# A hybrid decoder layer on one core: attention's first head begins two steps later in TensorE's order

## The chip, the core and the metric

The kernel runs on one core of one Trainium2 chip. The time is the device time of one execution in microseconds (us), the median of several runs. TensorE (PE in the profile) does the matrix products, VectorE (DVE) and ScalarE (ACT) the elementwise work and the reductions, GpSimd (POOL) a few small operations, and SyncE (SP) issues nearly all DMA transfers.

## The reference

One layer of a decoder on 512 tokens of width 1024. One input projection feeds three groups of heads side by side, their outputs are joined by one output projection, and a gated channel mixer follows:

```python
h = _rmsnorm(x, attn_norm[l])
proj = h @ w_in[l]
p_nsa, p_rw, p_moba = _split(proj, [N_IN_NSA, N_IN_RWKV, N_IN_MOBA])
o_nsa = _head_rmsnorm(_nsa_mixer(p_nsa, ...), nsa_out_gain[l])
o_rw = _rwkv7_mixer(p_rw, ...)
o_moba = _head_rmsnorm(_moba_mixer(p_moba), moba_out_gain[l])
x = x + jnp.concatenate([o_nsa, o_rw, o_moba], axis=-1) @ w_out[l]
x = x + _conv_glu(_rmsnorm(x, ffn_norm[l]), ffn_w_in[l], ...)
return _rmsnorm(x, final_norm)
```

The first group (six heads of 64) is attention with a selected, a windowed and a compressed branch; at 512 tokens the selected and the windowed branch are both plain causal softmax attention, with keys `ks` and `kw`. The second (four heads) is a recurrence with a matrix state, done in chunks of 64 tokens. The third (six heads) is block-sparse attention.

## The kernel before

All work of the first half is written as streams, Python generators that emit instructions and then `yield` a number. `merge` (L1035) keeps a due time for every stream, takes the stream that is due first and can go on, lets it emit one step, and adds the number that it yields to its due time (L1049). A stream that yields `None` is waiting for a condition and is tried again. The instructions so emitted, in this order, are the written order of every engine's queue; the order seen in the trace can differ from it by a little where instructions of two steps are mixed. The numbers are the planner's own units: a projection group of three products yields `CW` = 1.25, an attention step `CATT` = 2.5, a step of the recurrence 3.45 or 3.57 (or half).

The streams that matter here:

- `w_stream` (L1091) does the input projections in the order of `ORDER`: ..., `nv`, `q0`, `cv`, `ck`, `hv`, `q1`, `kw`, ... Each projection is eight groups of three products (`mm3`, L240 to L242: the operands are split into a high and a low part, `whi` and `wlo` for the weights, and three of the four products are summed). A weight unit is split by ScalarE (L211) and VectorE (L212). After the eighth group the result is taken from PSUM; for `q0` that is `evac_q` (L694): VectorE scales it into P (L696), ScalarE rounds it to the high part of the query tile `qt` (L701) and VectorE computes the low part (L702). `cv` and `ck` are taken over by `blocks` (L881), and `hv` is the product `ph` (L917, L918) that uses the blocks of `cv`.
- `rw_pair` (L347) is the recurrence, for two pairs of heads. Its steps here: the small products of L455 with the masks GA and GR that VectorE puts on them (L461, then NM, R and Nc); the inverse of 16 by 16 blocks on VectorE (L494, L496), which goes out and comes back through DMA (L503, L505) and is spread to DvT and Dv (L508); the products of L533 with Y (L573).
- `att_stream` (L1239) goes through `HEADS`: nine items of two halves (`par`). A half waits for its query, keys and values (L1252), and then `soft` (L774) emits four steps, one for each 128 tokens: two products into the bank `s` (L784, L785), the row minimum on VectorE (L788), the exponential on ScalarE (L791), and `yield CATT`. The first half of the first item needs `q0`, the second half needs `q1`, which comes after `cv`, `ck` and `hv`.

PSUM has eight banks; a step that needs one waits with `want` until the count of live banks allows it.

Of the kernel before, what the change touches and what calls it, by code (L numbers as in the profile page):

```python
# [24 lines left out]
CW, CRW0, CRW1, CATT, CVAL, CFIN, CCMP, CCA, RWLAG = 1.25, 3.45, 3.57, 2.5, 1.28, 4.05, 3.17, 1.69, 0  # L25
# [66 lines left out]
def hybrid_layer(ctx: ExitStack, tc: tile.TileContext, xT, cst, cols, lora, fgain, wA, wVn, cw1,  # L92
# [10 lines left out]
    def mark(label):  # L103
        MARKS.append((label, nc.cur_bb.bb.instructions[-1].name))
# [18 lines left out]
    def r2(name, shape=(128, 512), dt=F32):  # L123
        return sb.tile(list(shape), dt, name=name, bufs=cap(name))
# [135 lines left out]
    for z in SEQ:  # L260
# [13 lines left out]
        for k, i in new:  # L274
            n = sum(o[1] == i for o in order1)
# [498 lines left out]
    def soft(qt, kk, par, sums, mid):  # L774
        kh, kl, lo = kk
        two, three = r2("prob"), r2("prob")
        pt_ = two[:, 384:512], mid[:, par * 256:par * 256 + 256], two[:, 0:384], three
        Ps = []
        for i in range(NT):
            n = (i + 1) * 128  # L780
            yield from want()
            s_ = bank("s")
            qs = slice(i * 128, (i + 1) * 128)
            pe.matmul(s_[:, 0:n], qt[:, qs], kh[:, 0:n], start=True, stop=False)  # L784
            pe.matmul(s_[:, 0:n], qt[:, qs], kl[:, 0:n], start=False, stop=True)  # L785
            P = pt_[i]
            m = sm("m", 1)
            dve.tensor_tensor_reduce(out=P, in0=s_[:, 0:n], in1=con("cmask")[:, 512 - n:512], scale=1.0,  # L788
                                     scalar=3e38, op0=OP.add, op1=OP.min, accum_out=m)
            done()  # L790
            act.activation(P, P, AF.Exp, bias=m, scale=-1.0, accum_out=sums[:, i, par:par + 1])  # L791
            Ps.append(P)
            yield CATT
        return Ps
# [399 lines left out]
    def sums_tile():  # L1194
        return sm("sums", 8).rearrange("p (t h) -> p t h", h=2)
# [10 lines left out]
    def fin_nsa(j, b, OPt, sums, ob):  # L1206
        mark(f'fnsa{j}.{b}')
        c = sm("coef", 8)
        cv = c.rearrange("p (t h) -> p t h", h=2)
        dve.reciprocal(cv, sums)  # L1210
        o1 = 6 * j + b
        dve.tensor_tensor(cv, cv, gates[:, :, o1:o1 + 4:3], op=OP.mult)
        t = yield from scaled(OPt, c)
        ob.append(t)
        if len(ob) < 2:
            return
        while not cadone[0]:
            yield None
        yield CFIN
        at('ob').tensor_tensor(ob[0], ob[0], ob[1], op=OP.add)  # L1220
        yield from want()
        oc = bank("oc")
        for i in range(NT):
            pe.matmul(oc[:, i * 128:(i + 1) * 128], PT[j][:, i, :], Vbd[j], start=True, stop=True)
        yield CFIN
        dve.tensor_tensor(ob[0], ob[0], oc, op=OP.add)
        done()
        yield CFIN
        yield from finish_pair(ob[0], col("nsa_gain", j), j)

    def fin_moba(j, OPt, sums):
        mark(f'fmoba{j}')
        r = sm("coef", 8)
        dve.reciprocal(r, sums.rearrange("p t h -> p (t h)"))
        t = yield from scaled(OPt, r)
        yield CFIN
        yield from finish_pair(t, col("moba_gain", j), 5 + j)

    def att_stream():  # L1239
        for kind, j, b in HEADS:  # L1240
            fold = ENG[f"F{kind}{j}{b}"] == 'p'
            OPt, sums = (r2("OPt"), r2("OPt") if fold else None, fold), sums_tile()
            if b < 2:
                ob = []
            while len(queue) > QMAX:
                yield None
            Ps, vs, mid = [], [], r2("prob")
            for par in range(2):
                h = 2 * j + par
                if kind == "n":  # L1250
                    kk = (ks, kw)[b - 1]
                    while qn[h] is None or not kk or not vn:  # L1252
                        yield None
                    q_, k_, v_ = qn[h], kk[h // 3], vn[(b - 1) * 2 + h // 3]
                else:
                    while j not in mq or j not in mk or j not in mv:
                        yield None
                    q_, k_, v_ = mq[j][par], mk[j][par], mv[j][par]
                mark(f'soft{kind}{j}.{b}.{par}')
                vs.append(v_)  # L1260
                P = yield from soft(q_, k_, par, sums, mid)
                Ps.append(P)
            fin = fin_nsa(j, b, OPt, sums, ob) if kind == "n" else fin_moba(j, OPt, sums)
            queue.append((Ps, vs, OPt, fin, f'{kind}{j}.{b}'))
        queue.append(None)
# [14 lines left out]
    spawn(rw_run(0))  # L1280
    spawn(cmp_attention())
    spawn(att_stream())
    spawn(val_stream())
    merge()
# [267 lines left out]
```

## Time and profile before

| | |
|---|---|
| median of 3 runs | 731.04 us (730.73 to 731.48) |
| the profiled execution | 731.48 us, its span in the trace 729.4 us |
| TensorE busy | 705.4 us, 97% |
| VectorE busy | 627.0 us, 86% |
| ScalarE busy | 415.3 us, 57% |
| GpSimd busy | 30.8 us, 4% |

The busy shares are means over stages with different limits. The stage that the change touches is read by windows of time, by the waits of one engine, and by the order of time of one engine. In the order of time, a row gives start and duration in us, the engine, the line, the operation, the tile written and read, and how many records are merged; in brackets stands how long the engine was idle before it and what ended that.

### The profile page before, as it was taken

The page shows a single profiled execution, that of the slowest core. Times are in us where ns is not written, and L with a number is a line of the kernel's source. Part 1 is how long each engine was busy: PE and PEld are TensorE (multiplying, and loading weights), DVE is VectorE, ACT ScalarE, POOL GpSimd, SP SyncE. Part 2 cuts the span into 40 slices and gives each one's busy share as a digit, 9 for nine tenths or more (in the row PEclk, how much of TensorE's full clock was granted, in tenths as well). Part 3 has the DMA queues.
Part 4 walks back from the last instruction along what each step waited for, and adds up shares of the span by engine and source line. Part 5 has one row for each costly group of instructions (what it writes and reads, how often), then busy time and mean ns, then how long its engine had stood idle before and what let it go on. Part 6 is the DMA issues. An engine that isn't in the chain of part 4 may idle for free. (4 is left out here: it accounts for less than half of the span.)

```text
span 729.4 us, 13565 instructions
## 1 busy us (share of the span) xinstructions
PE 705.4 (97%) x5156; PEld 613.6 (84%) x5156; DVE 627.0 (86%) x1377; ACT 415.3 (57%) x862; POOL 30.8 (4%) x46
## 2 busy tenths in 40 slices
PE   9999988899999999999999999999999999999995
PEld 6777867678788788888899899999999999998884
DVE  6579679878897999797999999999999999999804
ACT  8475434465656877774766546455564555657403
POOL 4010100000000000011000000000000000000001
PEclk9989989999999999999999999999999999999999
DMA  9622021513110022024246333323333333346003
GB/s 328 193 87 80 13 50 49 140 65 117 44 44 30 1 59 73 30 72 145 74 144 218 97 107 102 116 87 102 97 108 101 102 103 110 98 126 201 1 1 115
DMA packets 44800, 69.86 MB, mean 96 GB/s; under 512 B 10688, under 2 KB 12352, under 8 KB 44736
## 3 DMA queue, kind: packets, MB, share of 16 engines
q1 hardware_dynamic: 44016, 67.95, 29.4%
q10 hardware_dynamic: 720, 1.06, 0.4%
q8 instruction: 40, 0.66, 0.4%
q14 instruction: 24, 0.20, 0.1%
HBM read 64.40 MB, written 4.59 MB: 95 GB/s over the span
## 5 line engine op out<-in xcount | busy, mean ns | idle before, releaser
L1301 ACT CAST ah<-S 128x512 fp32r<-128x512 f32 x88 | 54.5, 621 | 57.6 <-DVE S L1296 57.6
L240 PE MATMUL mm<-xh,whi 128*128 128x512 f32 x152 | 69.6, 458 | 0.0
L241 PE MATMUL acc<-dn,dn 128*128 128x512 f32 (+1 forms) x173 | 64.3, 372 | 0.0
L242 PE MATMUL acc<-dn,dn 128*128 128x512 f32 (+1 forms) x173 | 63.8, 371 | 0.0
L242 PE MATMUL mm<-xh,wlo 128*128 128x512 f32 x152 | 61.8, 406 | 0.0
L241 PE MATMUL mm<-xl,whi 128*128 128x512 f32 x152 | 61.5, 404 | 0.0
L1302 DVE TENSOR_TENSOR al<-S,ah 128x512 fp32r<-128x512 f32 x88 | 58.7, 682 | 0.7 <-ACT ah L1301 0.6
L791 ACT ACTIVATE prob<-prob,fixed 128x128 f32<-128x128 f32 (+1 forms) x72 | 40.5, 563 | 28.5 <-DVE fixed L788 26.5
L240 PE MATMUL acc<-dn,dn 128*128 128x512 f32 (+1 forms) x173 | 54.9, 371 | 0.0
L211 ACT CAST whi<-wraw 128x512 fp32r<-128x512 f32 x70 | 42.6, 618 | 19.8 <-PE mm L241 14.1
L212 DVE TENSOR_TENSOR wlo<-wraw,whi 128x512 fp32r<-128x512 f32 x70 | 47.3, 682 | 3.6 <-PE mm L242 2.2
L240 PE MATMUL pB<-bh,ah 128*128 128x256 f32 x172 | 50.1, 291 | 0.1
L242 PE MATMUL pB<-bh,al 128*128 128x256 f32 x172 | 48.6, 283 | 1.1 <-DVE al L1302 1.0
L242 PE MATMUL pC<-bh,al 128*128 128x256 f32 x172 | 48.5, 282 | 0.3 <-DVE al L1302 0.3
L240 PE MATMUL pC<-bh,ah 128*128 128x256 f32 x172 | 48.5, 282 | 0.2 <-ACT ah L1301 0.2
L241 PE MATMUL pB<-bl,ah 128*128 128x256 f32 x172 | 48.3, 281 | 0.0
L241 PE MATMUL pC<-bl,ah 128*128 128x256 f32 x172 | 48.1, 280 | 0.0
L1302 DVE TENSOR_TENSOR al<-wraw,ah 128x512 fp32r<-128x512 f32 x66 | 43.4, 681 | 0.0
L823 ACT CAST ph<-pt 128x512 fp32r<-128x512 f32 (+3 forms) x72 | 29.7, 425 | 23.3 <-PE pt L816 22.4
L788 DVE CUSTOM_DVE_ANT_0 prob<-s,early 128x128 f32<-128x128 f32 (+1 forms) x72 | 34.7, 483 | 6.6 <-PE s L785 5.0
L1301 ACT CAST ah<-wraw 128x512 fp32r<-128x512 f32 x66 | 36.8, 618 | 1.4 <-DVE x L1135 1.3
L241 PEld LDWEIGHTS acc<-dn,dn 128*128 128x128 f32 x173 | 32.6, 188 | 5.3 <-DVE dn L1365 0.2
(400 smaller groups left out, 2211.8 us busy)
## 6 DMA issues: line engine op xcount, KB each, us to landing
wraw<-in_wF_dram SPq DMA_DIRECT2D x88, 256.0 KB, 2.7
wraw<-in_wG_dram SPq DMA_DIRECT2D x44, 256.0 KB, 3.0
wraw<-in_wA_dram SPq DMA_DIRECT2D x38, 256.0 KB, 3.0
xr<-in_xT_dram SPq DMA_DIRECT2D x16, 256.0 KB, 4.1
wraw<-in_cw_dram SPq DMA_DIRECT2D x16, 256.0 KB, 3.3
wraw<-in_wO_dram SPq DMA_DIRECT2D x16, 256.0 KB, 2.6
fraw<-in_wA_dram SPq DMA_DIRECT2D x8, 256.0 KB, 5.2
x2d<-x2o SPq DMA_DIRECT2D x8, 256.0 KB, 3.3
```

Of the source, the lines that this page charges most:

```text
L211: act.copy(hi[:, :w], raw)
L212: dve.tensor_tensor(lo[:, :w], raw, hi[:, :w].bitcast(F32), op=OP.subtract)
L240: pe.matmul(o, ah, bh, start=first, stop=False)
L241: pe.matmul(o, ah, bl, start=False, stop=False)
L242: pe.matmul(o, al, bh, start=False, stop=last)
L788: dve.tensor_tensor_reduce(out=P, in0=s_[:, 0:n], in1=con("cmask")[:, 512 - n:512], scale=1.0, scalar=3e38, op0=OP.add, op1=OP.min, accum_ ...
L791: act.activation(P, P, AF.Exp, bias=m, scale=-1.0, accum_out=sums[:, i, par:par + 1])
L823: act.copy(h, t_[:, 0:n])
L1301: act.copy(h, src)
L1302: at(f'L{i}').tensor_tensor(l, src, h.bitcast(F32), op=OP.subtract)
```

## The change

When the first half of the first item has its operands, `att_stream` yields `2 * CATT` = 5.0 units once before it emits its first step. Nothing else is written differently, and no instruction is added or removed.

```diff
                     while j not in mq or j not in mk or j not in mv:
                         yield None
                     q_, k_, v_ = mq[j][par], mk[j][par], mv[j][par]
+                if (kind, j, b, par) == ("n", 0, 1, 0):
+
+                    yield 2 * CATT
                 mark(f'soft{kind}{j}.{b}.{par}')
                 vs.append(v_)
                 P = yield from soft(q_, k_, par, sums, mid)
```

## Rows read from the trace of the kernel before

**Rows 1.** Windows: length, busy us (records) per engine, granted clock, DMA share, GB/s.

```profile
92.60:140.00 47.40, 39.53 (x482) 31.89 (x483) 40.64 (x112) 19.72 (x44) 0.39 (x3) 0.89 0.25 66
140.00:700.00 560.00, 554.81 (x4043) 492.81 (x4042) 512.17 (x1092) 335.29 (x710) 14.96 (x9) 1.00 0.29 92
```

**Rows 2.** Waits of TensorE, 92 to 140 us: total us, times, longest.

```profile
PE s L784 <- DVE qt L702: 3.3, 1, 3.3
PE ph L918 <- DVE wlo L212: 2.5, 2, 2.1
PE rw L533 <- DVE Y L573: 1.7, 1, 1.7
...
```

**Rows 3.** TensorE in order of time, around the first head's first two steps.

```profile
92.19 0.38 PE L455 MATMUL rw<-AR,bb 64*64 64x128 f32 x2
95.91 0.47 PE L784 MATMUL s<-kk,qt 128*128 128x128 f32 x1 [3.34 <-DVE qt L702]
...
96.52 0.49 PE L455 MATMUL rw<-AR,bb 64*64 64x128 f32 x3
...
97.58 0.79 PE L240 MATMUL mm<-xh,whi 128*128 128x512 f32 x1
...
99.03 0.63 PE L240 MATMUL mm<-xh,whi 128*128 128x512 f32 x1
...
100.31 0.41 PE L784 MATMUL s<-kk,qt 128*128 128x256 f32 x1
...
100.86 1.59 PE L533 MATMUL rw<-DvT,R 64*64 64x64 f32 x32
```

**Rows 4.** VectorE in order of time, 86 to 105 us.

```profile
91.50 0.76 DVE L508 TENSOR_TENSOR DvT<-Nc,early 128x256 f32<-128x256 f32 x2 [4.78 <-DMA Nc<-s]
...
93.25 0.69 DVE L696 SCALAR_TENSOR_TENSOR P<-mm,early 128x512 f32<-128x512 f32 x1
...
95.17 1.41 DVE L702 TENSOR_TENSOR qt<-P,qt 64x512 fp32r<-64x512 f32 x2
...
97.69 0.42 DVE L461 TENSOR_TENSOR GA<-rw,early 128x256 f32<-128x256 f32 x1 [0.76 <-PE rw L455]
98.03 0.41 DVE L461 TENSOR_TENSOR GR<-rw,early 128x256 f32<-128x256 f32 x1
...
100.97 0.42 DVE L788 CUSTOM_DVE_ANT_0 prob<-s,early 128x256 f32<-128x256 f32 x1 [1.53 <-PE s L785]
...
104.44 0.42 DVE L461 TENSOR_TENSOR GA<-rw,early 128x256 f32<-128x256 f32 x1 [2.10 <-PE rw L455]
```

**Rows 5.** Windows, columns as in rows 1: behind the stall, VectorE's full stretch, its end.

```profile
97.60:100.30 2.70, 2.70 (x9) 2.13 (x7) 1.75 (x5) 0.00 (x0) 0.00 (x0) 0.50 0.00 0
...
104.40:131.40 27.00, 22.50 (x301) 18.41 (x301) 25.59 (x71) 10.74 (x26) 0.39 (x3) 1.00 0.17 45
...
131.50:134.70 3.20, 3.20 (x43) 2.59 (x43) 3.20 (x13) 2.70 (x6) 0.00 (x0) 0.67 0.52 161
```

**Rows 6.** TensorE in order of time, the same kinds of work at full clock.

```profile
60.01 0.45 PE L455 MATMUL rw<-AR,bb 64*64 64x128 f32 x8
...
61.05 0.50 PE L240 MATMUL mm<-xh,whi 128*128 128x512 f32 x1
...
105.12 0.34 PE L784 MATMUL s<-kk,qt 128*128 128x384 f32 x1
...
105.47 0.39 PE L240 MATMUL mm<-xh,whi 128*128 128x512 f32 x1
...
107.41 1.15 PE L533 MATMUL rw<-Dv,QT 64*64 64x64 f32 x32
108.49 0.50 PE L240 MATMUL mm<-xh,whi 128*128 128x512 f32 x1
...
109.29 0.40 PE L240 MATMUL mm<-xh,whi 128*128 128x512 f32 x1
...
109.98 0.39 PE L240 MATMUL mm<-xh,whi 128*128 128x512 f32 x1
```

## What the change should do to the time

> **What bounds the kernel now.** I read the table by stages first, to see which engine is full and where. From 140 to 700 us TensorE is busy 554.81 of 560.00 us at full clock [rows 1]: whatever time TensorE is ahead when it reaches 140 it keeps, because the work behind it is the same and is fed by engines that are ahead by the same amount. From 92.6 to 140 it is busy only 39.53 of 47.40, at a mean clock of 0.89. So the stage around the first head is where idle TensorE time can be removed.
>
> Second, the waits of TensorE in that stage. The longest, 3.3 us, is the first head's first product (L784), which waits for the query tile qt; the others are 2.5 for weights' low parts (wlo) and 1.7 for Y, all on VectorE [rows 2].
>
> Third, TensorE's order of time. After 18 of the 32 small products of the second recurrence pair (L455; 92.19 is the last of these rows) it stands still until 95.91, then does the first head's product, and only then the other 14 (96.52 is their first row) [rows 3]. Those 14 and the projection behind them do not need qt. The clock in the stretch after it is 0.50, the 1.2 GHz level [rows 5], and a group of three projection products takes 1.45 there (97.58 to 99.03) against 0.80 and 0.69 at full clock (108.49 to 109.29 to 109.98) [rows 3, 6].
>
> Fourth, why qt is late: VectorE's own order of time. It sits 4.78 us on a DMA that brings the inverse back for the first pair, then works off what queued up behind: DvT, Dv, P of the query at 93.25, and qt, which ends at 95.17 + 1.41 = 96.58 by the merged row (its first half is what TensorE waits for) [rows 4].
>
> **The change, part by part.** The yield puts the first head's stream 2 x 2.5 = 5.0 planner units later. A projection group costs 1.25 of them, so the four steps move by four groups each: the first step goes to where the third was (105.12), the second to where the fourth was, and the other two among the first groups of the next projection. The second half of this head waits for q1, which lies well beyond; from there the stream is again at its old place. So just four steps move.
>
> Each moved step issues two products on TensorE, a row minimum with its read on VectorE, an exponential with its read on ScalarE. No DMA is among them, so SyncE's and GpSimd's queues are not passed. Nothing is added or removed: the gain or loss is in waits and clock only.
>
> *TensorE, removed.* The stall, 3.34 by the row of L784 [rows 3]. Then the slow stretch after it: two projection groups 1.45 + 1.28 instead of 0.80 + 0.69, the 32 products of L533 1.59 instead of 1.15, the remaining 14 of L455 1.06 instead of 14/32 of 1.04 = 0.46 [rows 3, 6]: 5.38 - 3.10 = 2.28. The two moved products took 0.61 and 0.55; a larger one at full clock takes 0.35 (105.12 to 105.47), so they are cheaper by 0.46 in their new places. Together 3.34 + 2.28 + 0.46 = 6.1 us.
>
> *TensorE, does the first product wait again?* In the new order TensorE stands at 92.6 with 0.46 of L455, then two groups (0.80, 0.69), L533 (1.15), a group (0.80), the second L455 set (1.04), a group (0.80): it comes to the first product at about 98.3. The query is ready at 96.6, so 1.7 us of cover. If VectorE were later by more than that, the wait would return with the excess only. The second L455 set would stand at 96.5; should it get the PSUM banks of the first, it waits until VectorE has read these, about 96.6 + 4 x 0.34 = 98.0 (the spacing 97.69 to 98.03 and on). That is bounded by 0 and 1.5; I take 0, since it is less than TensorE's surplus over VectorE below.
>
> *VectorE, which decides how much of 6.1 survives.* In 104.4 to 131.4 VectorE is busy 25.59 of 27.00, and it is TensorE that waits [rows 2, 5]. So in that stretch TensorE's lead is cut down to VectorE's. VectorE is not faster before 96.6: its backlog runs without an idle time from P to qt [rows 4]. What it gains is the idle time it had because TensorE stood or ran slowly: 0.76 before the first GA, 1.53 before the second row minimum, 2.10 before the second GA set [rows 4], 4.39 us. With the new order the first GA set is ready at 93, the second at 97.5, and both moved row minima come after products that TensorE does at 98.3 and some 2 us later, where VectorE still has GA, NM, R and weights to do. So I take all three as removed: 4.4. Bounds: if the row minimum still meets its product too early, 1.53 stays, and the gain is 2.9; if also the other idle time of the full stretch closed, 27.00 - 25.59 = 1.41, it is 5.8. The value is near the middle, and follows the three named waits.
>
> *ScalarE* is busy 10.74 of 27.00 there [rows 5]; the four exponentials cost nothing where they go, and their results are used only after q1. If that cover were gone they would cost their own time, under a microsecond each.
>
> **The sum.** The profiled execution took 731.48, its span 729.4. Span 729.4 - 4.4 = 725.0, plus the 2.1 outside it, 727.1; that execution lay 0.44 above the median 731.04, so the median after is **726.6**.
>
> What is late next: with 6.1 of lead on TensorE and 4.4 on VectorE, TensorE meets the wait for Y (1.7 now) about 1.7 us earlier in relation, and it grows to about 3.4.
>
> **The rivals.**
>
> *The clock falls at the longer wait.* The stall of 3.34 was followed by the 0.50 clock; the stretch that holds the wait of 1.7 shows 1.00, and the stretch from 131.5, right behind the wait of 2.1 for weights, shows 0.67 [rows 3, 5]. If the wait for Y grows to 3.4 the same fall would follow there, at the price just worked out, 2.28 + 0.46 = 2.7, and if none of it hid behind the later waits on VectorE, the result is 726.6 + 2.7 = **729.3**. Against it: there are 2.5 us of waits for weights on VectorE behind it [rows 2], in which a slow TensorE loses nothing. The Trainium skill, "TensorE: Matmul & The Clock Gate", section "HAM oscillation", says that an engine which idles while it waits for data is put back to half rate and starts its next work slow; the trace agrees (3.34 idle, then 0.50), and by that rule this rival, at 729.3, is the outcome.
>
> *All of TensorE's gain survives.* If VectorE's full stretch hides slack, for instance because what TensorE waits for can be done earlier in VectorE's queue: 731.0 - 6.1 = **724.9**. For it: 1.41 us idle in the stretch. Against it: 25.59 of 27.00 busy.
>
> *Nothing changes.* The product of L784 stands in the middle of the L455 set, so the finished order is not only the written one; what places it may put it early again, before qt is ready: **731.0**. Against it: L784 would then have to pass four projection groups that are ready.
>
> *Slower.* VectorE's queue is served in order. If a moved row minimum stands there ahead of its product, everything behind it (GA, NM, blocks, weights) waits, in the stretch where VectorE decides. The price of one such meeting is the 1.53 that the second row minimum shows now; all four would cost 6.1, of which 4.4 is paid by the gain: 731.0 + 1.7 = **732.7**. It decides from four meetings of 1.1 on; below that the kernel is still faster. Against it: TensorE is 1.7 ahead of VectorE in the new order, so products come first.
>
> **How the numbers follow.** Forecast 726.6 (its own range, from 2.9 and 5.8: 725.2 to 728.2): 0.58. All survives, 724.9: 0.12. Clock, 729.3: 0.13. Nothing, 731.0: 0.08. Slower, 732.7: 0.09. The range leaves out the last two and little at the lower end: 724.5 to 729.6, 0.8 in all. A measurement of this kernel tells about 0.2%, 1.5 us, from no change: faster below 729.6 is 0.58 + 0.12 + somewhat over half of the clock case, 0.78; same is the rest of that and the fourth case, 0.13; slower 0.09.
>
> **What would show it.** Right: L455 with its 32 products unbroken before 93; L784 first at some 98 with no wait on qt; clock 1.00 from 92.6 to 105; VectorE without the 0.76, 1.53 and 2.10; TensorE's wait for Y longer than 1.7; the first group of q1 some 4.4 earlier than now; the same distances from there to the end. Wrong: a wait at L784 or at the second L455 set; new idle time of VectorE ahead of a row minimum; a clock below 1 behind the wait for Y; or a lead at q1 that is lost later, between 140 and 420.

## The result, and the profile after

The kernel after takes 725.67 us (median of 6 runs, 724.04 to 726.89), the kernel before on the same chip 730.47 (6 runs, 728.79 to 731.48): a ratio of 0.9938, 95% interval 0.9923 to 0.9954. The gain is 4.8 us; forecast were 4.4. The profiled execution of after took 725.59, its span is 723.5. Single executions of one kernel differ by several microseconds (the kernel before ran from 726.6 to 732.8 in all its executions), so below a time is a median, and what an edit did is read from the stage where it lies.

That stage can be measured between two marks that stand in every kernel: the last products ahead of the stage (the second pair's L433) and the products with Dv of the second pair (L533), behind the first head. First TensorE of the kernel before, then of the kernel after; columns are start, duration, engine, line, operation and tile, count, and in brackets the wait with what ended it.

```profile
90.04 1.02 PE L433 MATMUL rw<-rb__956,early 128*128 128x512 f32 x2
...
148.19 1.15 PE L533 MATMUL rw<-Dv,QT 64*64 64x64 f32 x32
```

```profile
88.94 1.02 PE L433 MATMUL rw<-rb__956,early 128*128 128x512 f32 x2
...
91.30 0.40 PE L455 MATMUL rw<-AR,kb 64*64 64x128 f32 x8
...
95.19 0.45 PE L455 MATMUL rw<-AR,bb 64*64 64x128 f32 x8
...
97.02 0.22 PE L784 MATMUL s<-kk,qt 128*128 128x128 f32 x1
...
99.58 0.38 PE L784 MATMUL s<-kk,qt 128*128 128x256 f32 x1 [0.80 <-DVE fixed L788]
...
112.80 1.96 PE L533 MATMUL rw<-TA,Y 64*64 64x128 f32 x32 [1.62 <-DVE Y L573]
...
124.77 0.38 PE L918 MATMUL ph<-wlo,bhl 128*128 128x256 f32 x1 [2.27 <-DVE wlo L212]
...
141.50 1.15 PE L533 MATMUL rw<-Dv,QT 64*64 64x64 f32 x32
```

The stage is 148.19 - 90.04 = 58.15 us long before and 141.50 - 88.94 = 52.56 after: 5.6 shorter. After was 1.1 ahead already at the first mark, which is no work of the change. The set of L455 runs through, the first head's first product at 97.02 waits for nothing, and a new wait stands ahead of the second step's product: 0.80 for the row minimum of the first step.

The waits of TensorE from 92 to 140 us in after, to be set against [rows 2]: the 3.3 is gone, the other two are as they were.

```profile
PE ph L918 <- DVE wlo L212: 2.7, 2, 2.3
PE rw L533 <- DVE Y L573: 1.6, 1, 1.6
PE s L784 <- DVE fixed L788: 0.8, 1, 0.8
...
```

VectorE of after in the same stretch answers [rows 4]. It still waits 4.72 us for the inverse, but from there on no row has a wait: the first GA follows qt at once, the second set follows a weight unit, and the first row minimum stands behind it.

```profile
90.39 0.76 DVE L508 TENSOR_TENSOR DvT<-Nc,early 128x256 f32<-128x256 f32 x2 [4.72 <-DMA Nc<-s]
...
91.97 0.68 DVE L696 SCALAR_TENSOR_TENSOR P<-mm,early 128x512 f32<-128x512 f32 x1
...
93.88 1.41 DVE L702 TENSOR_TENSOR qt<-P,qt 64x512 fp32r<-64x512 f32 x2
95.30 0.42 DVE L461 TENSOR_TENSOR GA<-rw,early 128x256 f32<-128x256 f32 x1
...
97.91 0.41 DVE L461 TENSOR_TENSOR GA<-rw,early 128x256 f32<-128x256 f32 x1
...
99.24 0.28 DVE L788 CUSTOM_DVE_ANT_0 prob<-s,early 128x128 f32<-128x128 f32 x1
```

Windows of after, columns as in [rows 1]. Where the clock was 0.50 [rows 5] it is 1.00, and the whole stretch to 140 has 0.96 for 0.89 (0.93 in a second trace of before, below). Only behind the wait of 2.27 for a weight is it still low (0.66 from 125 to 130, before 0.67).

```profile
92.60:140.00 47.40, 41.91 (x525) 33.11 (x525) 44.59 (x123) 22.51 (x48) 0.38 (x3) 0.96 0.31 85
...
97.60:100.30 2.70, 1.90 (x18) 1.22 (x18) 2.70 (x10) 0.50 (x2) 0.00 (x0) 1.00 0.00 0
92.60:105.00 12.40, 11.60 (x135) 8.76 (x136) 12.29 (x31) 6.04 (x12) 0.00 (x0) 1.00 0.14 34
...
125.00:130.00 5.00, 5.00 (x49) 4.10 (x49) 4.92 (x17) 2.69 (x6) 0.00 (x0) 0.66 0.57 179
```

### The profile page after: what moved, and what is told of

It is laid out like the page before. It is cut to its first block, busy times and chain, and to the rows that moved or that the text cites. A ratio compares the mean times of both kernels' runs of the same rounds, so it can differ in the third digit from the quotient of the medians.

```text
span 723.5 us, 13563 instructions
## 1 busy us (share of the span) xinstructions
PE 701.6 (97%) x5156; PEld 610.4 (84%) x5156; DVE 626.7 (87%) x1377; ACT 415.5 (57%) x862; POOL 30.4 (4%) x46
## 4 chain that ended last, share of the span: by engine, by line
PE 72%; DVE 16%; ACT 4%; DMA 4%; issue 2%; POOL 1%; SPq 0%; POOLq 0%; DVEq 0%; ACTq 0%
PE mm L240 6%; PE mm L241 6%; PE mm L242 6%; PE acc L241 5%; PE acc L242 5%; PE acc L240 5%; PE pB L240 3%; PE ot L804 3%; PE pB L242 3%; PE pB L241 2%; PE pC L240 2%; PE pt L816 2%; PE pC L241 2%; PE pC L242 2%; PE pA L241 2%; PE pA L242 2%
```

## The experiments

Times are medians of the kernel, of the kernel before measured beside it, and their ratio with its interval. The stage is the length between the two marks in the profiled execution.

| kernel | time | before | ratio | stage |
|---|---|---|---|---|
| before | | | | 58.15 |
| before, again | 730.29 | 729.34 | 1.0008 [0.9989, 1.0026] | 57.41 |
| after | 725.67 | 730.47 | 0.9938 [0.9923, 0.9954] | 52.56 |
| after, again | 725.38 | 729.66 | 0.9938 [0.9919, 0.9958] | 52.54 |
| one step | 724.09 | 730.45 | 0.9912 [0.9894, 0.9930] | 55.03 |
| one step, again | 725.07 | 729.66 | 0.9929 [0.9905, 0.9953] | 55.49 |
| four steps | 726.96 | 730.45 | 0.9956 [0.9939, 0.9973] | 54.57 |
| before, stall filled with products | 728.31 | 730.45 | 0.9970 [0.9957, 0.9984] | 55.83 |
| before, first DvT and Dv on GpSimd | 724.59 | 730.45 | 0.9922 [0.9907, 0.9937] | 51.68 |
| after, first DvT and Dv on GpSimd | 723.89 | 729.66 | 0.9919 [0.9898, 0.9941] | 51.41 |
| after, both pairs' DvT and Dv on GpSimd | 723.40 | 729.59 | 0.9915 [0.9895, 0.9934] | 52.54 |
| after, half of the block sums on GpSimd | 724.74 | 729.66 | 0.9928 [0.9908, 0.9949] | 52.06 |
| after, three more additions on VectorE | 729.27 | 729.59 | 0.9997 [0.9979, 1.0015] | 55.60 |
| before, the same three additions | 727.22 | 729.59 | 0.9964 [0.9948, 0.9980] | 56.46 |

**Both kernels once more.**

> The changed kernel once more, for a comparison on the same chip as the one-step delay. Expected as measured, 4 to 5.5 us faster than before.

> The kernel before, unchanged, once more, for a second trace of it: the other kernels' traces run 0.6 to 2.5 us ahead of the first trace of it already at 90 us, ahead of the place of the change, and the kernel before with additions on VectorE came out 2.4 us faster than without. Theory (the stall and the half clock behind it belong to the order, and how long each lasts differs from execution to execution with the return of the inverse by DMA): this trace too has a wait for qt of 2.8 to 3.4 us at the first product and a stretch of clock below 1.00 behind it, and its lead over the first trace at 138 us stands where it stood at 90 us, give or take 1.7 us (the length of the slow stretch). Rival (the slow stretch is a rare event of the first trace): the wait is there, the clock behind it is 1.00 throughout, and the lead grows by 2.0 us or more between 90 and 105 us.

After repeats itself: 52.54 for 52.56 us. Before does not quite. TensorE of its second execution, and the clock behind the stall (window, TensorE busy, granted clock, DMA share, GB/s):

```profile
95.24 0.35 PE L784 MATMUL s<-kk,qt 128*128 128x128 f32 x1 [3.98 <-DVE qt L702]
...
99.54 1.15 PE L533 MATMUL rw<-DvT,R 64*64 64x64 f32 x32
```

```profile
97.00:98.00 1.00, 1.00 (x3) 0.50 0.00 0
...
99.00:100.00 1.00, 1.00 (x19) 1.00 0.00 0
```

The stall is longer (3.98 for 3.34, above the 2.8 to 3.4 expected), the slow stretch shorter: the products of L533 take 1.15 here and took 1.59 [rows 3]. From the first product to the third it is 9.21 us in the first trace (95.91 to 105.12 [rows 3, 6]) and 8.11 in this one (95.24 to 103.35). The same work in the same order at full clock stands in the kernel with the first DvT and Dv on GpSimd (below); its first and third product:

```profile
91.21 0.33 PE L784 MATMUL s<-kk,qt 128*128 128x128 f32 x1 [0.53 <-DVE qt L702]
...
97.81 0.34 PE L784 MATMUL s<-kk,qt 128*128 128x384 f32 x1
```

That is 6.60, so the half clock cost 2.6 and 1.5 us in two executions of one kernel. The stall's own length goes with the DMA: the inverse is sent out and fetched back, and the second issue follows the first by 3.45 us in the first trace, by 3.87 in this (84.26 to 88.13), and by 3.09 in before with additions (below), where the stall is 2.92; it is 3.26 and 3.06 in the two of after. The theory of this run holds: stall and slow stretch belong to the order, their lengths do not. The mean of the two stages, 57.8, is the better base: the change shortens the stage by 5.2.

**One step and four instead of two.**

```diff
-                    yield 2 * CATT
+                    yield CATT        (four steps: 4 * CATT)
```

> The stream waits one step (2.5 units) instead of two; the rest is as in the changed kernel. My theory (the query tile comes late because VectorE's queue stands behind a DMA, and what TensorE gains is kept as far as VectorE gains): TensorE reaches the first product 1.3 to 1.5 us before the query is ready, so a wait of about that length comes back, too short for the clock to fall; VectorE still loses its three idle times (0.76, 1.53, 2.10), so nearly all the gain stays: 3.5 to 5 us faster than before, at most 1 us behind the changed kernel. Rival (TensorE's own time is what counts): the returned wait is paid in full, 1.4 us slower than the changed kernel.

> The one-step delay once more. In its first trace the wait for the query came back with 1.84 us and the clock fell behind it, and that execution was the slowest of its six. If the fall of the clock is by chance at a wait of this length, a second trace may show the wait with the clock at 1.00 and the time near the median of the first (724.1), even with or 1 us ahead of the changed kernel; if it falls at every wait of this length, the trace shows 0.50 again and the time is 1 to 2 us behind the changed kernel.

> The stream waits four steps (10 units). My theory: the query is ready long before, no wait is left to remove, so the time is that of the changed kernel within 1 us. Rival (the place of the steps counts in itself, the later the better or the worse): another 2 us or more in either direction.

With one step the first product still comes too early, and the clock falls behind its wait, which the first expectation had ruled out. TensorE of the second of these runs, and its window behind the wait (columns as in [rows 1]):

```profile
94.19 0.33 PE L784 MATMUL s<-kk,qt 128*128 128x128 f32 x1 [2.04 <-DVE qt L702]
...
96.92 0.71 PE L455 MATMUL rw<-AR,bb 64*64 64x128 f32 x8
```

```profile
96.00:98.00 2.00, 2.00 (x23) 1.35 (x25) 1.76 (x6) 0.81 (x3) 0.00 (x0) 0.50 0.03 8
```

Both traces have the wait (1.84 and 2.04) and the half clock behind it, and a stage 2.5 to 2.9 us longer than after's. Farther on both wait 1.92 for Y. What follows that wait differs; TensorE and a window of the first trace, then of the second:

```profile
116.05 3.57 PE L533 MATMUL rw<-TA,Y 64*64 64x128 f32 x32 [1.92 <-DVE Y L573]
...
117.00:119.00 2.00, 2.00 (x24) 2.00 (x22) 1.97 (x7) 0.58 (x1) 0.12 (x1) 0.50 0.09 35
```

```profile
114.92 1.96 PE L533 MATMUL rw<-TA,Y 64*64 64x128 f32 x32 [1.92 <-DVE Y L573]
...
116.00:118.00 2.00, 2.00 (x30) 1.69 (x24) 1.94 (x8) 1.65 (x3) 0.13 (x1) 1.00 0.02 8
```

One kernel, one wait of the same length, and once the half clock, once the full. The 1.6 us that L533 takes longer do not show in the stage (55.03 for 55.49): TensorE waits 1.0 less for weights behind it (2.2 for 3.2).

Yet the times of the two series are not longer than after's (ratio 0.9912 and 0.9929 against 0.9938, the intervals overlap), so neither case of the second expectation came in whole. Part of the difference lies behind the stage (below, in the step on the distances to the end). And the traced execution of the first series is not a typical one: it is the slowest of its six (726.58), with a mean granted clock of 0.990, where the other five have 0.994 or 0.995 and take 722.55 to 725.36. Whether those had the slow stretches no trace shows. Which of the two delays is better the times do not tell.

With four steps the first product waits for nothing, and the queue of steps falls later instead, among the block products. TensorE and a window of that kernel:

```profile
111.16 0.43 PE L917 MATMUL ph<-whi,bhl 128*128 128x256 f32 x1 [1.78 <-DVE stmp L494]
...
112.67 3.68 PE L533 MATMUL rw<-TA,Y 64*64 64x128 f32 x32 [0.65 <-DVE Y L573]
```

```profile
115.00:118.00 3.00, 3.00 (x22) 2.67 (x19) 2.81 (x8) 1.32 (x3) 0.00 (x0) 0.50 0.00 0
```

TensorE reaches the block products and Y sooner than VectorE has them, waits 1.78 and 0.65 us, and the clock falls: L533 with TA takes 3.68 for 1.96 in after. That is the prediction's rival of the clock, with another wait than the one that it named. The stage is 2.0 us longer than after's, where no difference was expected, and the ratio 0.9956 is the smallest gain of the delays.

**Stall or clock: the stall filled.** The kernel before, with 14 products ahead of the first head's product, whose result nobody reads:

```diff
+                if (kind, j, b, par) == ("n", 0, 1, 0):
+                    yield from want()
+                    fill = bank("s")
+                    for _ in range(14):
+                        pe.matmul(fill, xh[0][:, 0:128], vn[0].rearrange("p t a d -> p t (a d)"), start=True, stop=True)
+                    done()
```

> The order of before, with 14 products of 512 columns that nobody reads put in front of the first head's first product (3.2 us at full clock), so that TensorE works while the query is late. It takes the clock's share of the gain from the stall's. My theory: the stall goes to under 1 us of idle, the clock stays at 1.00, the work itself is not done earlier at the stall but is not slowed after it; the slow stretch costs 2.3 to 2.7, of which VectorE lets 1 to 2.5 through: 728 to 729.5 with before at 730.5. Rival (the fall of the clock costs nothing, only the stall does): as before or up to 0.6 us slower. Rival (the clock is nearly all of it): as the changed kernel.

TensorE of it:

```profile
89.36 3.43 PE L1263 MATMUL s<-vn,xh 128*128 128x512 f32 x14
93.45 0.33 PE L784 MATMUL s<-kk,qt 128*128 128x128 f32 x1 [0.66 <-DVE qt L702]
```

The useful work comes hardly earlier, and all 32 products of L455 now stand behind the first product, where before has 14 of them; but the clock is 1.00 there, and the stage falls from 57.8 to 55.8. That agrees with the 2.6 and 1.5 found above for the half clock, 2.1 in the mean. So about 2 of the 5.2 us are the clock's; the stage of after is 3.3 shorter than this one, and that part needs useful work in the stall's place. The times differ by 2.1 as well (730.45 to 728.31), but that is no second proof: in this trace the first mark comes 0.9 and 2.2 earlier than in the two of before, and the rest behind the stage is 1.3 longer (582.5), both outside the stage.

**The cause ahead of the stall.** The order of before, but DvT and Dv of the first pair, which wait for the DMA, on GpSimd:

```diff
-        for src, dst, eng in ((XX, DvT, dve), (X, Dv, at('dv'))):
+        for src, dst, eng in ((XX, DvT, dve if p else pool), (X, Dv, dve if p else pool)):
```

> The order of before, but the four products that spread the returned inverse of the first pair to DvT and Dv run on GpSimd, so VectorE does not stand behind their DMA. My theory: the query's P starts at about 90.2 instead of 93.25, qt is ready for the first product at about 92.5, the wait of 3.3 shrinks to under 1 us, the clock stays at 1.00, and the kernel is 4.5 to 7 us faster than before with every step in its old place. Rival (what counts is where the steps stand in TensorE's order): within 1 us of before.

VectorE and GpSimd of it, in order of time:

```profile
88.36 0.69 DVE L696 SCALAR_TENSOR_TENSOR P<-mm,early 128x512 f32<-128x512 f32 x1 [3.43 <-PE mm L242]
```

```profile
90.00 1.63 POOL L508 TENSOR_TENSOR DvT<-Nc,early 128x256 f32<-128x256 f32 x2 [9.45 <-DMA Nc<-s]
```

P now waits for its own operand, not behind the DMA; the wait at the first product is 0.53, the clock 1.00, the stage 51.7 (6.1 shorter), the time 5.9 below before. So qt was late because P stood behind DvT on VectorE; with that cured, the order of before is as good as the new one. The 6.1 are not the wait's alone: the edit also takes four operations, two rows of 0.76 us [rows 4], off VectorE.

The change and this edit together:

> The changed kernel with DvT and Dv of the first pair on GpSimd as well, so both remedies for the same wait at once. My theory (both take away the same wait): the two gains don't add; TensorE has no wait left to lose at the first product, VectorE is rid of four short products (1.4 us) and of 1 us of backlog: 0 to 2 us faster than the changed kernel, 724 to 726. Rival (two separate gains): they add, 4.8 + 5.9, about 720.

The stage is 51.4, 0.3 shorter than with the edit alone and 1.1 shorter than with the change alone. The gains do not add (5.2 and 6.1 would be 11.3), as expected of two remedies for the same idle time.

**Who decides behind the stall: more work for VectorE.** Three additions of 512 columns behind the first GA and GR of the second pair, whose result nobody reads, in after and in before:

```diff
-                done()
+                done(); [dve.tensor_tensor(r2('pad', (128, 2, 2, 2, CH)), GA[0], GR[0], op=OP.add) for _ in range(3 * p * par * (2 - c0) // 2)]
```

> The changed kernel with three additions of 512 columns added on VectorE, behind the first GA/GR set of the second pair; nobody reads their result, and all else stands in the same order on every engine. By the rows of other 512-column operations they cost 0.60 to 0.68 us each, 1.8 to 2.0 together. Theory (since the change VectorE has no idle time between 92 and 131 us, and its order of work there sets how early the second half comes): VectorE is later by 1.8 to 2.0 us from there, TensorE's waits for VectorE (Y, wlo) take that up, the lead over the kernel before falls from 5.6 to 3.6 to 3.8 us by 138 us, and the time is 1.5 to 2.0 above that of the changed kernel, about 727.2. Rival (what was won is TensorE's alone, VectorE had room left): the lead stays at 5.2 or more and the time within 0.5 of 725.4.

> The kernel before with the same three additions on VectorE at the same place, behind the first GA/GR set of the second pair; nobody reads their result. Theory: the additions stand where VectorE waits 2.10 us for the second GA/GR set, so that wait shrinks to 0.1 to 0.3 us, what follows from 104.4 us on is where it was, and the time is that of the kernel before within 0.5 us (730.0 to 731.0); together with the same additions in the changed kernel (1.5 to 2.0 us there) this says that the idle time of VectorE, and not TensorE's alone, is what the change won. Rival (additions on VectorE cost the same wherever they stand): 1.8 to 2.0 us slower, 732.3.

In after: VectorE, then TensorE.

```profile
95.41 0.68 DVE L464 TENSOR_TENSOR pad<-GA,GR 128x512 f32<-128x512 f32 x1
...
102.50 0.69 DVE L573 TENSOR_TENSOR Y<-rw,Dv 128x512 f32<-128x512 f32 x1 [0.79 <-PE rw L533]
```

```profile
99.83 0.50 PE L784 MATMUL s<-kk,qt 128*128 128x256 f32 x1 [2.36 <-DVE fixed L788]
...
100.47 1.97 PE L533 MATMUL rw<-Dv,QT 64*64 64x64 f32 x32
```

In before: VectorE at the second GA set.

```profile
99.95 0.69 DVE L464 TENSOR_TENSOR pad<-GA,GR 128x512 f32<-128x512 f32 x1
100.55 0.42 DVE L461 TENSOR_TENSOR GA<-rw,early 128x256 f32<-128x256 f32 x1
```

The additions take 1.8 us (three of 0.60, from start to start). In before they lie in the wait of 2.10 ahead of the second GA set, which is gone in this trace: the stage is 56.5, not longer than before's 58.2 and 57.4, as the theory had it. In after the stage grows by 3.0, more than their own 1.8: the row minimum of the first step comes later, TensorE's wait for it grows from 0.80 to 2.36, the clock falls (L533 takes 1.97 for 1.15), and VectorE then waits for TensorE in its turn (0.79, and 0.62 for cP). So VectorE had idle time there before the change and has none after it: that idle time is what the change won.

Both expectations of time missed. After with the additions is 3.6 to 3.9 us slower than after (1.5 to 2.0 expected); the extra is the new waits with the clock, and 0.9 behind the stage (582.97 us from the second mark to the end). Before with the additions is not level with before but 2.4 us faster. Its trace shows a shorter stall (2.92) and a short slow stretch (8.11 from first to third product, as in before's second trace), and 1.4 less behind the stage (579.7 for 581.1), which goes back to one wait for a transfer far from the additions (below, in the step on the distances to the end). A stage 1.3 shorter and a rest 1.4 shorter are the gain; neither is shown to come from the additions.

**What bounds next.** Half of the block sums (L896) of after on GpSimd, `'blk': 'p'` for `'blk': 'v'` in the table of engines:

> The changed kernel with every second of the 16 additions at L896 (0.57 us each) on GpSimd: 8 x 0.57 = 4.6 us less for VectorE in its full stretch. My theory (VectorE decides what is kept there): TensorE's waits on VectorE in that stretch (1.6 for Y, 2.7 for weights) shrink and the kernel gets 1.5 to 4 us faster than the changed one. Rival (TensorE or the recurrence's chain decides): within 0.7 us of the changed kernel.

VectorE, GpSimd and TensorE of it:

```profile
109.26 0.57 DVE L896 TENSOR_TENSOR blk<-cP,fixed 64x248 f32<-64x248 f32 x1
109.76 0.66 DVE L496 TENSOR_TENSOR X<-X,stmp 64x39 f32<-64x39 f32 x1
110.45 1.07 DVE L896 TENSOR_TENSOR blk<-cP,fixed 64x248 f32<-64x248 f32 x1
```

```profile
108.86 2.30 POOL L896 TENSOR_TENSOR blk<-cP,fixed 64x248 f32<-64x248 f32 x2
```

```profile
135.13 1.15 PE L533 MATMUL rw<-DvT,R 64*64 64x64 f32 x32 [1.27 <-DVE DvT L508]
```

The waits for weights (2.7 in after) are gone, but the stage is only 0.5 shorter than after's and the time 0.6 below it, where 1.5 or more had been expected. While GpSimd works, operations of VectorE take 1.07 for 0.57 and 0.66 for 0.2; TensorE now waits 1.27 us for the second pair's inverse, and longer than in after for the first row minimum (1.16 for 0.80). The lengthened rows and the recurrence's chain with its round trip by DMA are what stands against the gain; the share of each is not shown.

DvT and Dv on GpSimd for both pairs, in the changed kernel (`pool` for both engines in the line above):

> The changed kernel with the spreads DvT and Dv (L508) on GpSimd for both pairs, so VectorE waits for neither return of an inverse by DMA. With the first pair alone on GpSimd the lead was 6.7 us. Theory (VectorE's order of work decides, and its second wait for the DMA of 1.9 us at 134 us blocks P of the second head too): up to 1.9 us more, if TensorE's waits for wlo and for DvT behind 128 us don't take it: a lead of 7 to 8.5, time 722 to 724. Rival (behind 130 us TensorE waits for the inverse itself, which GpSimd spreads 0.9 us later than VectorE would): lead as with the first pair alone, 6.2 to 6.8, time 723.5 to 724.5, or less than that if the DvT products wait for GpSimd.

The stage is 52.5, not shorter than with the first pair alone (51.4): the second head's first product, which waited for nothing there, waits 0.6 us for qt, and the theory of a further gain falls. The median, 723.40, is the lowest of all kernels, 6.2 below before, but its interval overlaps those of the first pair alone on GpSimd, of the same edit in before, of one step and of half of the block sums: these fastest versions can't be told apart.

## Why the prediction held, step by step

**Bound and mechanism: right.** From 140 to 700 us TensorE is busy 554.91 of 560.00 us, as in [rows 1]; the gain comes from the stage ahead. The L455 set is unbroken until 91.30 + 0.40, L784 comes first at 97.02, without a wait; before's frame is 1.1 later, so 98.1 for the 98.3 of the prediction. The cover of 1.7 us is there: qt's row ends at 93.88 + 1.41 = 95.29.

**TensorE, removed (6.1): the mechanism right, the size that of one execution.** The stall of 3.34 and its slow stretch are gone. But 2.28 + 0.46 = 2.7 for the half clock was one execution's figure; 2.6 by the marks used above in that trace, it is 1.5 in another trace of the same kernel, whose stall is longer (3.98).

**No wait at the second L455 set: right. No wait at the second step: wrong.** The set at 95.19 waits for nothing. The prediction said that both moved row minima come where VectorE still has GA, NM and R to do; it did not go on to ask what waits for a row minimum that stands behind them. It is the second step's product: 0.80.

**VectorE, 4.4: right, too low by 1.0 for the trace that it was read from.** VectorE's part of the weight for which TensorE waits longest, first before, then after:

```profile
130.74 0.68 DVE L212 TENSOR_TENSOR wlo<-wraw,whi 128x512 fp32r<-128x512 f32 x1
```

```profile
124.04 0.68 DVE L212 TENSOR_TENSOR wlo<-wraw,whi 128x512 fp32r<-128x512 f32 x1
```

VectorE is 6.70 ahead here and was 93.25 - 91.97 = 1.28 ahead at P: 5.4 won, near the upper bound of 5.8. The three named waits are gone (0.76, 1.53, 2.10), and with them small ones that the prediction left standing, 0.19 for TensorE and 0.53 for ScalarE in the full stretch; 5.11 in all. The other 0.3 are in no wait. In the second trace of before the three named waits are 0.66, 1.00 and 1.63, and against it 4.3 are won (36.38 us from P to this row, 32.07 and 32.09 in the two traces of after).

**What is late next (Y, 1.7 to 3.4): wrong.** The wait for Y is 1.62. TensorE's 6.1 is cut by the new 0.80 to 5.3, VectorE won as much, so the distance between them stays. For the same reason the rival of the clock did not come in after; by four steps and by VectorE's additions it did, and in one trace of one step at the very wait for Y. There its 1.6 us cost the stage nothing, as the prediction had said of a slow TensorE ahead of VectorE's later waits.

**The same distances to the end: nearly.** The rest of the kernel behind the second mark, span less mark, is 581.2 and 581.0 us in the two traces of before, 582.0 and 582.2 in those of after: 1.0 is lost again. Most of it goes at 512 us, in the channel mixer. ScalarE there, in the kernel after:

```profile
512.15 0.62 ACT L1367 CAST dn<-wraw 128x512 fp32r<-128x512 f32 x1 [1.39 <-DMA wraw<-in_wG_dram]
```

Such waits for weights stand in every kernel (4.7 us of them behind 420 us in before) and mostly cost nothing. This one is passed on: VectorE waits 0.88 for ScalarE, and TensorE, busy without a gap from 420 to 530 us in both traces of before, is busy 109.69 of 110.00 there, in the second trace of after 109.24. Why this transfer comes late in after no run here tells.

In other kernels the rest differs at an earlier place, the start of the channel mixer near 385 us. ScalarE there, in before, in before with the stall filled, and in before with additions:

```profile
389.92 0.62 ACT L1364 CAST dn<-wraw 128x512 fp32r<-128x512 f32 x1 [2.69 <-DMA x2d<-x2o]
```

```profile
386.60 0.62 ACT L1370 CAST dn<-wraw 128x512 fp32r<-128x512 f32 x1 [3.98 <-DMA x2d<-x2o]
```

```profile
384.19 0.62 ACT L1364 CAST dn<-wraw 128x512 fp32r<-128x512 f32 x1 [1.13 <-DMA wraw<-in_wG_dram]
```

This row stands 241.7, 243.0 and 240.1 us behind the second mark, and the rests are 581.2, 582.5 and 579.7: nearly the whole difference is this one wait for a transfer. With one step it is 1.48 and 1.54, and the rest 580.2 and 580.0, which is part of why those kernels are no slower. So times that differ by 1 to 3 us need not differ by the stage; why these transfers land earlier or later is open.

So 5.2 less 1.0 is 4.2 by the traces, beside 4.8 and 4.3 by the two pairs of medians. The prediction took the rest as fixed, with 4.4 for the stage: a term too low by 0.8 and a missing one of 1.0 nearly cancel. That the time came so near is in part luck.

**Rivals.** "All of TensorE's gain survives" comes near for the stage (5.2 to 5.6 of 6.1), not for the time. "Nothing changes" and "slower" are out: no moved row minimum waits for its product.

## What to carry to other kernels

Where an engine stalls on an operand, ask first what that operand stands behind: here an unrelated operation that waits for a DMA in a queue served in order, and moving that operation or moving the consumer gave nearly the same. A stall's price is its own length and the clock behind it, and it is kept only as far as the engine that is late next has idle time to give up: count all its idle rows, the small ones too. Delay the consumer just past its operand; with four steps for two the waits came back farther on, and the stage was 2.0 us longer. Compare stages and not times alone: executions of before differ by up to 6.2 us, more than the gain.

## What the runs showed of the hardware

- The clock fell to 0.50 behind waits of 1.84 and 2.04 us (one step) and was 1.00 behind the 1.62 for Y in after. Behind the same wait of 1.92 it was 0.50 in one trace of the one-step kernel and 1.00 in another. The longer wait had not the longer slow stretch: 3.98 us cost 1.5, 3.34 cost 2.6. The Trainium skill, "TensorE: Matmul & The Clock Gate", section "HAM oscillation", has an engine that waits for data put back to half rate and its next work start slow; the traces agree for most of these waits, and show that the length of the wait alone gives neither the fall nor its price.
- Executions of before that took longer had the lower mean granted clock: the ten shortest of 65 (726.6 to 728.5 us) have 0.991 to 0.993, the ten longest (731.8 to 732.8) 0.983 to 0.988. The one behind the rows of before (731.48) has 0.986.
- The round trip of the inverse, the same code and the same bytes, took from 3.06 to 3.87 us between its two issues.
- VectorE's operations took up to 1.07 for 0.57 us while GpSimd worked on the same kind of sums. The Trainium skill, "SBUF — State Buffer", section "SBUF: two separate sides", says that the two share a port and that the later one is held up; the lengthened rows agree.
